# GpSimd kept in emission order, and the sixth product's weight splits two groups ahead, in a two-layer trunk kernel

## The chip, the cores and the metric

The kernel runs on one core of a Trainium2 chip. The metric is the device time of one launch in microseconds (us). The core's engines are TensorE (PE in the rows, PEld for its weight loads), VectorE (DVE), ScalarE (ACT), GpSimd (POOL) and SyncE (SP). DMAs are issued from an engine's instruction stream; those that GpSimd issues go through one queue, q0, and those of SyncE through q1.

## The reference

Two layers over 512 tokens of width 1024, in f32. Each layer makes one wide projection of the normed input, three token mixers (pooling, retention, attention into 256 memory tokens), merges them by gates, and ends with an output projection and a squared-ReLU MLP of width 4096:

```python
h = rms_norm(x, norm_mix_g[l])
proj = h @ w_in[l]
pool_u, rq, rk, rv, rg, xq, gates = split(proj)
y_pool = pool_mixer(pool_u, ...)
y_ret = retention(rq, rk, rv, rg, ...)
y_mem = memory_attention(xq, rms_norm(mem, mem_norm_g[l]), w_mem_kv[l])
merged = sum of sigmoid(gate_b) * (y_b @ w_up_b[l])
x = x + merged @ w_out[l]
h2 = rms_norm(x, norm_mlp_g[l])
x = x + square(relu(h2 @ w_mlp1[l])) @ w_mlp2[l]
```

## The kernel before

**Products.** Every big projection is a 1024x1024 weight against the 512 tokens, cut into 2x2 blocks, and computed with seven block products instead of eight. The code numbers them, and `products` (L293) runs them in the order 1, 2, 5, 3, 6, 4, 7. Each has two groups, for the two halves of the contraction; "4.1" here is product 4, second group. A layer runs, in this order, the projections v (with the first product of the next one taken ahead), qk, three gates (g1, g2, g0), the memory keys and values, rg, xq, three smaller up-projections without this scheme, w_out, and then four chunks of the MLP, each an mlp1 and an mlp2 projection.

**A group** takes a 512 KB weight tile `raw`, splits it into a high part (`wh`, a cast on ScalarE, L114) and a low part (`wl`, a subtraction on VectorE, L117), and multiplies with an operand that is split in the same way (`x6h` and `x6l` are the parts of product 6's operand; L104 and L105). Three matmuls stand for one (L123 to L125: wh with xh, wh with xl, wl with xh), so a group is 12 matmuls of 512 columns, or 24 of 256.

**Weights.** The weight's blocks are in three tiles per half, called A, C and B in the code. Sums of blocks are made in place by DMAs that add to SBUF, which GpSimd issues in `take`. After the splits 1.0 and 1.1 block (0,1) is added to A, after 5.0 and 5.1 block (1,1) is added to A, and after 3.0 and 3.1 block (0,1) is added to B (all L236). Product 6 takes A, and its `take` also adds A to C (L238, `raw<-raw`, SBUF to SBUF); product 4 takes that C. `skip` (L219) makes the first pair of adds where product 1 was done ahead. The plain loads of A, C and B are on SyncE's queue.

**Order.** `push` puts a group in a list; `prepare` emits the weight split of every group that is at most `look` places from the front, LOOK = 3 (2 for product 4). `MANUAL` names the engines whose instructions stay in the order in which the code emits them. It holds TensorE alone; on ScalarE, VectorE and GpSimd a scheduler sets the order when the program is built. `prep` emits a group's weight split, and after it the split of the operands that are to be had by then (`x.get`), or puts them on the list `wanted`. GpSimd also computes the inverse square roots of the norms (`pow`, L557): `yss` of retention's heads, which all come at the start of rg, `mr` of the memory, and `r` of the rows of `x`.

Of the kernel before, what the change touches and what calls it, by code (L numbers as in the profile page):

```python
# [2 lines left out]

# [13 lines left out]
ET = mybir.EngineType  # L17
# [16 lines left out]
MAGIC = 12582912.0  # L34
NSLOT = 72
LOOK = 3
MANUAL = {ET.PE}


C_CNT = 0  # L40
# [28 lines left out]
def tile_trunk(ctx, tc, a, out):  # L69
# [7 lines left out]
    psum = ctx.enter_context(tc.tile_pool(name="psum", bufs=8, space=PSUM))  # L77
    ctx.enter_context(tc.manual_schedule(engines=MANUAL))

    def slot(shape=(P, T), dt=F32, name="t"):  # L80
        return slots.tile(list(shape), dt, tag="t", name=name)

    def bank(name="ps"):
        return psum.tile([P, T], F32, tag="ps", name=name)
# [35 lines left out]
    def mm(ps, stat, mov, start, stop):  # L120

        (sh, sl), (mh, ml) = stat, mov
        nc.tensor.matmul(ps, sh, mh, start=start, stop=False, skip_group_check=True)  # L123
        nc.tensor.matmul(ps, sh, ml, start=False, stop=False, skip_group_check=True)  # L124
        nc.tensor.matmul(ps, sl, mh, start=False, stop=stop, skip_group_check=True)  # L125
# [15 lines left out]
    wanted = []  # L141
    follows = {1: (2,), 2: (5,), 5: (3, 4), 3: (6,), 6: (7,)}
# [17 lines left out]
    def prepare():  # L160
        for i, w in enumerate(queue):
            if w[0] and i <= w[2]:
                w[1], w[0] = w[0](), None

    def step():
        nonlocal post
        settle()
        _, state, _, go = queue.pop(0)
        post = go(state)
        prepare()  # L170

    def push(prep, go, look=LOOK):
        queue.append([prep, None, look, go])
        prepare()
        if len(queue) > LOOK:
            step()
# [6 lines left out]
    def urgent(f, *args):  # L183
        with tc.high_priority(offset=4000):
            return f(*args)
# [107 lines left out]
    def products(x, done, fm=False, last=False, acc=None, ahead=None):  # L293
# [9 lines left out]
        w, nxt = plan[at], plan[at + 1] if at + 1 < len(plan) else None  # L303
# [2 lines left out]
        ps = {}  # L306
        sb = {}

        def prep(p, kp, w=w):
            def f():  # L310
                wp = w.take(p, kp)
                for q in (p or 1, *follows.get(p, ())):
                    if x.have(q, kp):
                        for k in range(kp + 1):
                            if x.have(q, k):
                                x.get(q, k)
                    elif q == (p or 1):
                        wanted.append((x, q, kp))
                        break
                return wp  # L320

            return f

        def go(p, kp, into, new, fm=fm, then=None):
            def f(wp):
                if kp == 0 and new:
                    ps[into] = [bank(f"P{into}") for _ in range(2)]
                xp = x.get(p, kp)
                bs = ps[into]
                if fm:  # L330
                    for c in range(4):
                        o = bs[c // 2][:, (c % 2) * H:(c % 2 + 1) * H]
                        for k in range(2):
                            mm(o, tuple(v[:, k, c * P:(c + 1) * P] for v in wp), tuple(v[:, k, :] for v in xp),
                               new and kp == 0 and k == 0 and c % 2 == 0, kp == n - 1 and k == 1 and c % 2 == 1)
                else:
                    for b in range(2):
                        for k in range(2):
                            mm(bs[b], tuple(v[:, k, b * P:(b + 1) * P] for v in xp), tuple(v[:, k, :] for v in wp),
                               new and kp == 0 and k == 0, kp == n - 1 and k == 1)  # L340
                if kp == n - 1 and then:
                    return then
                if kp == n - 1:
                    return lambda: urgent(after, p) if p in (5, 6) or last and p in (3, 7) else after(p)

            return f
# [62 lines left out]

        def product(p, into=None):  # L410
            for kp in range(n):
                push(prep(p, kp), go(p, kp, into or p, into is None), LOOK - 1 if p == 4 else LOOK)

        def product_ahead(k, its_fm):
            its = plan[at - 1 + k]

            def then():
                for b in range(2):
                    u = slot(name="u2")
                    nc.scalar.copy(u, ps["ahead"][b])  # L420
                    early.setdefault(its, []).append(u)

            its.ahead()
            for kp in range(n):
                push(prep(0, kp, its), go(1, kp, "ahead", True, its_fm, then))

        if w.early:
            until(lambda: len(early.get(w, ())) == 2)
            for b, u in enumerate(early.pop(w)):
                sb["u", b] = u  # L430
            w.skip()
        else:
            product(1)
        if ahead:
            product_ahead(*ahead)
        product(2)
        if nxt:
            nxt.load("A")
        product(5)
        product(3)  # L440
        product(6, 5)
# [25 lines left out]
    def plain(xs, done):  # L467
# [33 lines left out]
        for c in range(2):  # L501
            for kp in range(n):
                push(prep(c, kp), go(c, kp))
# [271 lines left out]
    for l in range(DEPTH):  # L775
# [346 lines left out]
        def up_done(branch, first=False, final=False):  # L1122
# [17 lines left out]
            return done  # L1140

        products(hop, v_done, ahead=(1, True))
        products(hop, rotated, fm=True)
        sides.append(mixing())
        products(hop, gate_done(1))
        products(hop, gate_done(2))
        sides.append(memory())
# [141 lines left out]
```

## Time and profile before

| | |
|---|---|
| median of 3 runs | 1690.19 us (1690.08 to 1692.25) |
| the profiled execution, its own time | 1697.43 us |
| its span | 1695.4 us |
| mean granted TensorE clock | 0.986 of full |
| TensorE busy | 1614.6 us (95%) |
| VectorE busy | 1262.7 us (74%) |
| ScalarE busy | 1034.7 us (61%) |
| GpSimd busy | 313.6 us (18%) |

Shares are of the whole span, and stages with different limits lie in them. Busy time of GpSimd contains what it takes to issue a DMA, not the transfer. In the timelines below each row gives its start, its length, the engine, the line, the operation, what is written and read, and in brackets the engine's idle time before it and what ended that. A row of a `wh` cast that waits for `DMA raw<-raw` waits for the landing of an L238 copy into C.

### The profile page before, as it was taken

To read this page: it belongs to the slowest core of one execution; us is meant where nothing else is said; L and a number is where in the kernel's file an instruction comes from. 1 tells how busy PE (TensorE), PEld (TensorE's weight loads), DVE (VectorE), ACT (ScalarE), POOL (GpSimd) and SP (SyncE) were. 2 spreads that over 40 slices of the span, in tenths; PEclk is the share of its full clock that TensorE was granted. 3 is DMA by queue.
4 is the path that set the end of the run, shared out by engine and by line. 5 is a ranking of instruction groups with operands and counts; after the bars stand their busy time and mean duration, and the time that the engine had idled before them with its cause. 6 is when DMAs were issued, how large, how long until landed. Compare 5 with 4: busy or idle time off the path is not lost. (4 is left out here: it accounts for less than half of the span.)

```text
span 1695.4 us, 24850 instructions
## 1 busy us (share of the span) xinstructions
PE 1614.6 (95%) x9354; PEld 1419.1 (84%) x9354; DVE 1262.7 (74%) x1727; ACT 1034.7 (61%) x1655; POOL 313.6 (18%) x292
## 2 busy tenths in 40 slices
PE   6799999999989899999989999999999889999997
PEld 5697888998878888989868888889888688989895
DVE  4787675767687788696976876757757779796868
ACT  6456776646357656565765577756543577566565
POOL 2112212200012122222231223022000212222221
PEclk9999999999999899999999999999999999999999
DMA  8699986873666788988887999778435779888875
GB/s 237 148 229 235 251 211 148 183 232 103 193 128 126 162 195 178 197 189 207 180 200 159 241 242 244 218 169 181 151 115 162 173 160 186 194 177 189 174 151 123
DMA packets 155256, 311.16 MB, mean 184 GB/s; under 512 B 11320, under 2 KB 12544, under 8 KB 155136
## 3 DMA queue, kind: packets, MB, share of 16 engines
q0 software_dynamic: 61440, 134.23, 46.6%
q1 hardware_dynamic: 83872, 159.42, 28.0%
q10 hardware_dynamic: 9824, 15.93, 2.6%
q8 instruction: 73, 1.20, 0.3%
q14 instruction: 47, 0.39, 0.1%
HBM read 255.01 MB, written 16.78 MB: 160 GB/s over the span
## 5 line engine op out<-in xcount | busy, mean ns | idle before, releaser
L117 DVE TENSOR_TENSOR wl<-raw,wh 128x1024 fp32r<-128x1024 f32 x496 | 603.3, 1221 | 290.4 <-ACT wh L114 287.1
L114 ACT CAST wh<-raw 128x1024 fp32r<-128x1024 f32 x496 | 519.4, 1051 | 488.9 <-PE P L125 120.9
L236 POOL DMA_DIRECT2D raw<-in_w_mlp x92 | 121.6, 1352 | 386.3 <-DVE wl L117 250.2
L236 POOL DMA_DIRECT2D raw<-in_w_in x80 | 104.9, 1371 | 364.5 <-DVE wl L117 227.3
L238 POOL DMA_DIRECT2D raw<-raw x64 | 57.6, 900 | 168.9 <-DMA raw<-in_w_mlp 73.3
L1175 DVE TENSOR_TENSOR x<-x,P 128x512 f32<-128x512 f32 x120 | 78.3, 678 | 3.6 <-PE P L125 3.4
L123 PE MATMUL P<-wh,x6h 128*128 128x512 f32 x160 | 64.5, 403 | 10.4 <-ACT x6h L104 7.1
L123 PE MATMUL P<-wh,x3h 128*128 128x512 f32 x160 | 64.2, 401 | 10.0 <-ACT x3h L104 10.0
L125 PE MATMUL P<-wh,x6l 128*128 128x512 f32 x160 | 64.5, 403 | 4.3 <-DVE x6l L105 4.3
L236 POOL DMA_DIRECT2D raw<-in_w_out x12 | 15.9, 1461 | 275.6 <-DVE wl L117 156.1
L125 PE MATMUL P<-wh,x5l 128*128 128x512 f32 x160 | 63.5, 397 | 2.8 <-DVE x5l L105 2.8
L123 PE MATMUL P<-wh,x1h 128*128 128x512 f32 x160 | 64.1, 401 | 2.0 <-ACT x1h L104 2.0
L124 PE MATMUL P<-wl,x4h 128*128 128x512 f32 x160 | 62.8, 392 | 2.7 <-DVE wl L117 2.7
L125 PE MATMUL P<-wh,x3l 128*128 128x512 f32 x160 | 64.2, 401 | 0.3 <-DVE x3l L105 0.3
L124 PE MATMUL P<-wl,x6h 128*128 128x512 f32 x160 | 63.9, 399 | 0.6 <-DVE wl L117 0.6
L123 PE MATMUL P<-x6h,wh 128*128 128x256 f32 x192 | 56.5, 294 | 8.2 <-ACT P L368 8.2
L123 PE MATMUL P<-wh,x5h 128*128 128x512 f32 x160 | 63.3, 396 | 0.7 <-ACT x5h L104 0.5
L124 PE MATMUL P<-wl,x3h 128*128 128x512 f32 x160 | 63.8, 399 | 0.0
L123 PE MATMUL P<-wh,x7h 128*128 128x512 f32 x160 | 63.1, 394 | 0.5 <-ACT c L387 0.5
L124 PE MATMUL P<-wl,x1h 128*128 128x512 f32 x160 | 63.5, 397 | 0.0
L125 PE MATMUL P<-wh,x1l 128*128 128x512 f32 x160 | 63.2, 395 | 0.0
L123 PE MATMUL P<-wh,x4h 128*128 128x512 f32 x160 | 62.8, 393 | 0.1
(312 smaller groups left out, 5200.2 us busy)
## 6 DMA issues: line engine op xcount, KB each, us to landing
raw<-in_w_mlp SPq DMA_DIRECT2D x100, 512.0 KB, 5.0
raw<-in_w_mlp POOLq DMA_DIRECT2D x96, 512.0 KB, 7.6
raw<-in_w_in SPq DMA_DIRECT2D x88, 512.0 KB, 5.1
raw<-in_w_in POOLq DMA_DIRECT2D x84, 512.0 KB, 7.6
raw<-raw POOLq DMA_DIRECT2D x64, 512.0 KB, 6.8
sgl<-sig SPq DMA_DIRECT2D x48, 256.0 KB, 5.6
sig<-c ACTq DMA_DIRECT2D x36, 256.0 KB, 4.6
raw<-in_w_mem_kv SPq DMA_DIRECT2D x16, 512.0 KB, 5.5
```

What stands on the lines that cost most here:

```text
L114: nc.scalar.copy(hi, raw)
L117: nc.vector.tensor_tensor(lw, raw, hi.bitcast(F32), ALU.subtract)
L123: nc.tensor.matmul(ps, sh, mh, start=start, stop=False, skip_group_check=True)
L124: nc.tensor.matmul(ps, sh, ml, start=False, stop=False, skip_group_check=True)
L125: nc.tensor.matmul(ps, sl, mh, start=False, stop=stop, skip_group_check=True)
L236: nc.gpsimd.dma_start(raw, rows2(then, kp), accum_op=ALU.add)
L238: nc.gpsimd.dma_start(self.buf["C"][kp], raw, accum_op=ALU.add)
L1175: nc.vector.tensor_tensor(x, x, part, op)
```

## The change

GpSimd joins the engines that keep the order of emission. The weight splits of product 6 are emitted two groups ahead instead of three, as those of product 4 were already, and with them goes what `take` does after a split, the issue of the L238 DMA. The operand part of `prep` moves into a function of its own, which `push` runs when the group is put on the list, ahead of the weight split.

```diff
 LOOK = 3
-MANUAL = {ET.PE}
+MANUAL = {ET.PE, ET.Pool}
...
-    def push(prep, go, look=LOOK):
+    def push(prep, go, look=LOOK, first=None):
+        if first:
+            first()
         queue.append([prep, None, look, go])
         prepare()
...
+        def operands(p, kp):
+            for q in (p or 1, *follows.get(p, ())):
+                if x.have(q, kp):
+                    for k in range(kp + 1):
+                        if x.have(q, k):
+                            x.get(q, k)
+                elif q == (p or 1):
+                    wanted.append((x, q, kp))
+                    break
+
         def prep(p, kp, w=w):
-            def f():
-                wp = w.take(p, kp)
-                for q in (p or 1, *follows.get(p, ())):
...
-                return wp
-
-            return f
+            return lambda: w.take(p, kp)
...
-                push(prep(p, kp), go(p, kp, into or p, into is None), LOOK - 1 if p == 4 else LOOK)
+                push(prep(p, kp), go(p, kp, into or p, into is None), {6: 2, 4: 2}.get(p, LOOK), partial(operands, p, kp))
...
-                push(prep(0, kp, its), go(1, kp, "ahead", True, its_fm, then))
+                push(prep(0, kp, its), go(1, kp, "ahead", True, its_fm, then), LOOK, partial(operands, 0, kp))
```

The lines of the code move down by one to three: L236 becomes L239, L238 becomes L241, L557 becomes L558, L114 becomes L115.

On GpSimd in one mlp2 projection (layer 2, third chunk), from its first add to its last DMA; the tiles 15017 and 15019 are the halves of A, 15343 and 15345 those of B, 15215 and 15217 those of C. Before:

```order
L236 DMA raw_15017<-in_w_mlp2 128x2x512
L236 DMA raw_15019<-in_w_mlp2 128x2x512
L236 DMA raw_15017<-in_w_mlp2 128x2x512
L236 DMA raw_15019<-in_w_mlp2 128x2x512
L238 DMA raw_15215<-raw_15017 128x1024
L236 DMA raw_15343<-in_w_mlp2 128x2x512
L238 DMA raw_15217<-raw_15019 128x1024
L236 DMA raw_15345<-in_w_mlp2 128x2x512
```

And after the change:

```order
L239 DMA raw_15017<-in_w_mlp2 128x2x512
L239 DMA raw_15019<-in_w_mlp2 128x2x512
L239 DMA raw_15017<-in_w_mlp2 128x2x512
L239 DMA raw_15019<-in_w_mlp2 128x2x512
L239 DMA raw_15343<-in_w_mlp2 128x2x512
L239 DMA raw_15345<-in_w_mlp2 128x2x512
L241 DMA raw_15215<-raw_15017 128x1024
L241 DMA raw_15217<-raw_15019 128x1024
```

Both copies into C now stand behind both adds to B. The same holds in every projection of the scheme but xq, where the order was like this before.

On ScalarE in the same projection, after the change (before it, the rows stand in this order too), from the cast of 6.1 to that of 4.1:

```order
L115 CAST wh_15654<-raw_15019 128x1024
L105 CAST x4h_15534<-act_15462 128x512
L355 COPY u2_15543<-P1_15467 128x512
L355 COPY u2_15545<-P1_15468 128x512
L105 CAST x6h_15561<-xs6_15491 128x512
L115 CAST wh_15675<-raw_15215 128x1024
L105 CAST x6h_15582<-xs6_15526 128x512
L115 CAST wh_15693<-raw_15217 128x1024
```

Nothing moved here: the cast of 4.0, which reads C, stands ahead of the second `x6h`, as it did.

On GpSimd at the start of rg in the first layer; 2431 and 2433 are the halves of A. Before:

```order
L236 DMA raw_2431<-in_w_in 128x2x512
L557 TENSOR_TENSOR yss_2630<-yss_2630,nhalf_90 128x2
L236 DMA raw_2433<-in_w_in 128x2x512
L557 TENSOR_TENSOR yss_2680<-yss_2680,nhalf_90 128x2
L557 TENSOR_TENSOR yss_2732<-yss_2732,nhalf_90 128x2
L557 TENSOR_TENSOR yss_2766<-yss_2766,nhalf_90 128x2
L236 DMA raw_2431<-in_w_in 128x2x512
```

And after the change:

```order
L558 TENSOR_TENSOR yss_2630<-yss_2630,nhalf_90 128x2
L558 TENSOR_TENSOR yss_2680<-yss_2680,nhalf_90 128x2
L558 TENSOR_TENSOR yss_2732<-yss_2732,nhalf_90 128x2
L558 TENSOR_TENSOR yss_2766<-yss_2766,nhalf_90 128x2
L239 DMA raw_2431<-in_w_in 128x2x512
L239 DMA raw_2433<-in_w_in 128x2x512
L239 DMA raw_2431<-in_w_in 128x2x512
```

All four `yss` now stand ahead of the first add of rg. The order of TensorE and of SyncE is the same before and after.

## Rows read from the trace of the kernel before

**Rows 1.** The page's head, and its line of the weight subtractions (count, busy, mean ns).

```profile
span 1695.4 us, 24850 instructions
PE 1614.6 (95%) x9354; PEld 1419.1 (84%) x9354; DVE 1262.7 (74%) x1727; ACT 1034.7 (61%) x1655; POOL 313.6 (18%) x292
...
L117 DVE TENSOR_TENSOR wl<-raw,wh 128x1024 fp32r<-128x1024 f32 x496 | 603.3, 1221 | 290.4 <-ACT wh L114 287.1
```

**Rows 2.** Waits by engine and releaser: us in total, times, longest us.

```profile
PE P L123 <- ACT x3h L104: 11.1, 4, 6.4
PE P L123 <- ACT x6h L104: 7.1, 2, 3.8
PE P L125 <- DVE x6l L105: 4.3, 2, 2.4
...
ACT wh L114 <- DMA raw<-raw: 95.3, 33, 6.4
```

**Rows 3.** The page's DMA queues: packets, MB, share of 16 engines' span.

```profile
q0 software_dynamic: 61440, 134.23, 46.6%
```

**Rows 4.** Timeline, xq: GpSimd's first adds after 5.0; ScalarE's cast 4.0; both layers.

```profile
327.79 3.69 POOL L236 DMA_DIRECT2D raw<-in_w_in  x3 [9.64 <-DVE wl L117]
...
345.06 1.05 ACT L114 CAST wh<-raw 128x1024 fp32r<-128x1024 f32 x1 [6.36 <-DMA raw<-raw]
...
1159.17 3.68 POOL L236 DMA_DIRECT2D raw<-in_w_in  x3 [10.18 <-DVE wl L117]
...
1175.31 1.05 ACT L114 CAST wh<-raw 128x1024 fp32r<-128x1024 f32 x1 [5.42 <-DMA raw<-raw]
```

**Rows 5.** Timeline, mlp2, layer 2, third chunk: GpSimd, ScalarE, VectorE and TensorE.

```profile
1570.44 1.20 POOL L236 DMA_DIRECT2D raw<-in_w_mlp  x1 [7.29 <-DVE wl L117]
...
1585.21 1.07 ACT L114 CAST wh<-raw 128x1024 fp32r<-128x1024 f32 x1
...
1590.13 2.01 ACT L114 CAST wh<-raw 128x1024 fp32r<-128x1024 f32 x2 [3.34 <-DMA raw<-raw]
...
1588.63 0.68 DVE L105 TENSOR_TENSOR x6l<-xs,x6h 128x512 fp32r<-128x512 f32 x1
...
1590.20 0.39 PE L125 MATMUL P<-wh,x6l 128*128 128x512 f32 x1
```

**Rows 6.** Timeline, rg: GpSimd and TensorE in layer 1, then in layer 2.

```profile
281.66 0.69 POOL L557 TENSOR_TENSOR yss<-yss,nhalf 128x2 f32<-128x2 f32 x1 [1.88 <-DVE yss L556]
285.77 1.23 POOL L236 DMA_DIRECT2D raw<-in_w_in  x1 [3.43 <-DVE wl L117]
...
292.10 0.91 POOL L238 DMA_DIRECT2D raw<-raw  x1 [2.37 <-DMA raw<-in_w_in]
...
307.45 0.39 PE L124 MATMUL P<-wl,x4h 128*128 128x512 f32 x1
...
1113.24 0.69 POOL L557 TENSOR_TENSOR yss<-yss,nhalf 128x2 f32<-128x2 f32 x1 [1.95 <-DVE yss L556]
...
1138.83 0.39 PE L124 MATMUL P<-wl,x4h 128*128 128x512 f32 x1
```

**Rows 7.** Timeline, w_out of layer 2: GpSimd's add after 5.0, ScalarE's cast 4.0, TensorE.

```profile
1310.15 1.21 POOL L236 DMA_DIRECT2D raw<-in_w_out  x1 [14.34 <-DVE wl L117]
...
1328.06 1.04 ACT L114 CAST wh<-raw 128x1024 fp32r<-128x1024 f32 x1
...
1331.16 0.80 PE L123 MATMUL P<-wh,x6h 128*128 128x512 f32 x1 [3.79 <-ACT x6h L104]
```

**Rows 8.** Windows (window, length; busy us of PE, PEld, DVE, ACT, POOL; PEclk, DMA share, GB/s).

```profile
850.00:860.00 10.00, 7.78 (x43) 6.37 (x42) 8.24 (x13) 7.18 (x14) 3.15 (x3) 1.00 1.01 241
1331.00:1338.00 7.00, 4.94 (x11) 3.49 (x12) 6.78 (x11) 3.02 (x7) 0.00 (x0) 0.52 0.98 238
```

**Rows 9.** Timeline, between the layers: GpSimd's `r` and TensorE's first transpose behind it.

```profile
851.03 1.20 POOL L557 TENSOR_TENSOR r<-r,nhalf 128x2 f32<-128x2 f32 x1
...
853.41 0.76 PE L454 MATMUL tr<-ident,xn 128*128 128x128 f32 x5 [2.22 <-ACT xn L586]
```

More of the change, by code (lines that the diff above doesn't have):

```diff
@@ L2 @@
 from fractions import Fraction
+from functools import partial
 import concourse.bass as bass
@@ L307, in products @@
         sb = {}
-        def prep(p, kp, w=w):
-            def f():
-                wp = w.take(p, kp)
-                for q in (p or 1, *follows.get(p, ())):
[L313 to L319, printed above, removed]
-                return wp
-            return f
+        def operands(p, kp):
[7 more added lines that the diff above has]
+                    break
+        def prep(p, kp, w=w):
+            return lambda: w.take(p, kp)
         def go(p, kp, into, new, fm=fm, then=None):
```

## The prediction, made before the changed kernel ran

> **What bounds the kernel now.** The page's head first: TensorE is busy for 1614.6 of 1695.4 us [rows 1]. Its order does not change and nothing is taken from its work, so the change can only win or lose idle time of TensorE, 81 us in all, and the clock that goes with it. The list of waits says what of that is near this change [rows 2]: TensorE stands 11.1 us for `x3h`, 7.1 for `x6h` and 4.3 for `x6l`. The same list shows a wait that costs little so far: 33 of the 64 `wh` casts behind a C copy stand on ScalarE for it, 95.3 us in all. Last the queue: q0 is busy 46.6% of the span [rows 3], over 192 adds and 64 copies, so a transfer of 512 KB takes 0.466 x 1695.4 / 256 = 3.1 us of all 16 engines, and as GpSimd's transfers follow one another in it, what stands ahead of a copy is paid by who waits for the copy.
>
> **The change part by part.**
>
> Nothing is removed or added: the same instructions, with GpSimd's in another order. What moves are the C copies (L238). Before, most projections had them right behind the 5.0 and 5.1 adds or between the B adds; now both B adds come first. 4.0's cast, which reads C, waits for four adds and a copy behind 5.0's split. That arrangement is already there in xq, and there the time from the issue of 5.0's add to 4.0's cast, which ended a wait for the copy, was 345.06 - 327.79 = 17.27 us and 1175.31 - 1159.17 = 16.14 us [rows 4].
>
> *mlp2, eight times.* In the third chunk of layer 2 the 5.0 add is issued at 1570.44 and 4.0's cast starts at 1585.21 without a wait [rows 5]. Behind that cast on ScalarE stands the second `x6h`, and behind its subtraction on VectorE the second `x6l` (the order shows it for ScalarE; on VectorE it is the same in all mlp2 but the last of a layer). From the cast to the end of `x6l` it takes 1.05 + 1.22 + 0.68 = 2.95 us [rows 1, 4, 5], and TensorE wants `x6l` at 1590.20 [rows 5]. So the cast is harmless up to 1587.25. At xq's pace it comes at 1570.44 + 16.14 to 17.27 = 1586.58 to 1587.71: nothing to 0.5 us. The pace of this projection itself is another: 4.1's cast, which today has three adds and two copies ahead of it in q0, five transfers as 4.0's will have (four adds and its copy), came at 1590.13, 19.69 us behind the issue. By that 4.0 would be late by 2.9 us. I take 2.0, nearer to the projection's own row than to xq's, because the weight slices and the load on the queues are its own; in the last chunk of each layer, where `x6l` stands ahead of 4.0's subtraction, 1.2 less, 0.8. Sum 6 x 2.0 + 2 x 0.8 = **13.6 us** (0 to 20.8). mlp1 has its 4.0 cast due later relative to 5.0 (groups of 24 matmuls, and no second `x6h` held up that TensorE wants at once); I put it at nothing, and the same holds of g2, g0 and qk; what hides it there is the product 6 still running on TensorE, and if that cover were short by a microsecond in each of eight mlp1, 8 us would come on top.
>
> *rg, twice.* The four `yss` now stand ahead of rg's first add. The last one runs at 281.66 for 0.69, so 1.0's add is issued at 282.35 or later; 5.0's split must wait for it to land. An add there took 292.10 - 285.77 = 6.33 us to land, as the C copy waiting for it shows [rows 6]. Then come cast and subtraction, 1.05 + 1.22 = 2.27 us, and 5.0's add is issued at 290.95, not 285.77. With 17.27 us behind it 4.0's cast starts at 308.22. TensorE wants `wl` of 4.0 at 307.45, so the latest harmless start was 305.18: late by 3.0. In layer 2, 1113.24 + 0.69 + 6.33 + 2.27 + 17.27 = 1139.80 against 1138.83 - 2.27 = 1136.56: 3.2. Sum **6.3 us** (4.0 at 16.14, 11.2 at 19.69).
>
> *w_out, twice.* The 5.0 add is issued at 1310.15, 4.0's cast starts at 1328.06, `x6h` stands behind it, and TensorE waits 3.79 us for that [rows 7]. The 5.1 add, which waited behind a copy that itself waited for 5.0's landing, now goes earlier, but `x6h` will stand behind 4.0's cast all the same, at 1310.15 + 16.14, 17.27 or 19.69 = 1326.3, 1327.4 or 1329.8. That is -1.8, -0.7 or +1.8 each. I take +1.0, sum **+2.0** (-3.6 to +3.6).
>
> *v, g1, m10.* In the first layer's v the `x3h` stall of 6.4 us, the longest of its row [rows 2], stands behind a 6.1 cast that waits for the 5.1 add; that add now leaves before the copy, worth up to one transfer of 3.1 us: -2.5 (-5.3 to -1). In the second layer's v the second `x6h` moves behind 4.1's cast, one more copy of 3.1 us to wait for, part hidden: +1.5 (-1 to +3). g1's 4.0 is among the 33 waiting casts, of 2.9 us on average (95.3 / 33) [rows 2], half of that as my estimate for one layer: +1.5 (0 to 5.8). mlp1's first chunk (m10): 0 (-2.5 to +3). Sum **+0.5**.
>
> *`r`, three times.* Between layers, and from w_out to the MLP, `r` now stands ahead of an add issue. `r` ran at 851.03, 0.76 us after that issue began, on which it waited, and the first transpose behind it is what TensorE idled 2.22 us for [rows 9]: 3 x -0.76 = **-2.3**.
>
> *The clock.* From 1331 to 1338 the granted clock was 0.52, the 1.2 GHz level, behind two stalls of 3.79 and some 2 us [rows 7, 8]: 7 x 0.48 = 3.4 us lost. Behind the lone 2.22 us of the layer boundary it stayed at 1.00 [rows 8, 9]. So a stall of 2 us need not cost it and one of 4 may. I take half of the loss, 1.7, for each rg and for two of the eight mlp2: **+6.8** (0 to 17).
>
> Sum 13.6 + 6.3 + 2.0 + 0.5 - 2.3 + 6.8 = **+26.9 us**. The profiled execution took 1697.43 us, its span 1695.4 and 2.0 around it; that becomes 1724.3. It is 7.2 above the median of the runs, so the median goes from 1690.19 to **1717**. All low ends together give about -10 (1680), all high ends about +62 (1752).
>
> The trace gives 3.1 us for a transfer in q0 [rows 3]. The Trainium skill, "DMA: Bandwidth & Descriptors", section "Anatomy of one DMA — SWDGE (gpsimd) path", fits such a DMA at 2.0 us that don't grow plus its bytes over 436e3 per us; if the fixed part of one overlaps the next, 512 KB would be an estimated 1.2 us each and the two B adds 2.4 us together. By that the copies would hardly be later, and the time would go rival A's way; the trace's 3.1 us speaks against it.
>
> **The rivals.**
>
> *A, faster, about 1665.* The adds freed from the copies (5.1 no longer behind a copy that waits for 5.0) end the waits of TensorE for `x3h`, `x6h` and `x6l`, 11.1 + 7.1 + 4.3 = 22.5 us, and `r` brings 2.3: 1690.2 - 24.8 = 1665. Place: w_out, v and m10. It decides if the two B adds ahead of a copy cost it less than 1587.25 - 1585.21 = 2.0 us together, so that no 4.0 cast in mlp2 gets late. For it: these stalls are real and adds are in them. Against it: 3.1 us each by the queue's share, and xq's 16 to 17 us.
>
> *B, nearly unchanged, about 1692.* xq's faster pace holds everywhere: mlp2 0 to 4, rg 4 to 6, w_out -2, v -1, g1 0, `r` -2.3, no clock loss, +2 in the middle. This is also the case in which the move of product 6 has no effect of its own, since the order of ScalarE in mlp2 is what it was. For it: xq is the very arrangement. Against it: the mlp2 row of 19.69.
>
> *C, much slower, about 1741.* The projection's own pace holds: mlp2 6 x 2.9 + 2 x 1.7 = 20.8, rg 11.2, w_out 3.6, v and g1 +0.5, `r` -2.3, and the clock falls behind each of the ten stalls, 17: +50.8. For it: the fall after w_out. Against: no fall after 2.22 us.
>
> **How the numbers follow.** Forecast 0.58, A 0.16, B 0.12, C 0.14. About 0.2%, 3.4 us, is what a measurement of this kernel can tell from no change. Of B, 0.07 lies within that, 0.03 above and 0.02 below. Faster: 0.16 + 0.02 = 0.18; same 0.07; slower 0.58 + 0.14 + 0.03 = 0.75. The range reaches from the middle of B's band below, 1687, to 1748, above C's middle; it leaves out most of A and a part of C, some 0.2.
>
> **What would show it.** Right: ScalarE's wait of `wh` for `raw<-raw` well above 95.3 us; TensorE waiting some 2 us for `x6h` or `x6l` in each mlp2, about eight new waits, and for `wh` or `wl` of 4.0 in both rg; 4.0's casts in mlp2 starting 17 to 20 us behind the issue of the 5.0 add; the clock below 1.00 behind some of them; the transposes behind `r` idling 0.7 us less. Wrong: 4.0's casts in mlp2 without a wait and the `x3h` and `x6h` waits gone (A), or new waits of ScalarE that TensorE does not feel (B). It is also wrong if the stalls come somewhere else, in mlp1 above all, which I put at nothing.

## The result, and the profile after

The changed kernel takes 1751.59 us (median of four runs, 1748.0 to 1757.66) against 1691.22 us before: **3.5% slower**, ratio 1.0348 with a 95% interval of 1.0326 to 1.037. The forecast was 1717 us in 1687 to 1748. The sign was right, the loss more than twice as large as forecast (60.4 us between the medians, 26.9 forecast), and the median lies 3.6 us above the range.

The page of the profiled execution, its first lines and its queue line, for [rows 1] and [rows 3]:

```profile
span 1752.1 us, 24907 instructions
...
PE 1633.1 (93%) x9354; PEld 1427.9 (81%) x9354; DVE 1260.1 (72%) x1727; ACT 1034.4 (59%) x1655; POOL 315.0 (18%) x292
...
q0 software_dynamic: 61440, 134.23, 44.3%
```

The span grew by 56.7 us. TensorE's busy time grew by 18.5 of them although it does the same 9354 matmuls: a third of the loss is matmuls that run slower behind a stall. The other 38.2 us are idle time. The queue moves the same bytes. The waits, for [rows 2] (us in total, times, longest); the first line is one of before that [rows 2] does not have:

```profile
PE P L123 <- ACT P L368: 11.6, 4, 4.1
...
PE P L124 <- ACT P L369: 27.6, 4, 7.9
PE P L124 <- ACT x6h L105: 18.4, 10, 6.3
...
PE P L124 <- ACT wh L115: 8.9, 4, 2.9
PE mtr L958 <- ACT mnf L961: 8.6, 2, 4.3
PE P L125 <- DVE wl L118: 7.4, 6, 2.2
PE P L126 <- DVE x6l L106: 6.9, 8, 1.6
PE P L124 <- ACT x3h L105: 4.8, 3, 3.2
...
ACT wh L115 <- DMA raw<-raw: 181.0, 56, 8.4
```

56 of the 64 casts of product 4 now wait for their C copy, 181.0 us in all (33 casts and 95.3 us before). TensorE feels it in several forms: ten waits for `x6h` instead of two, eight for `x6l` instead of two, four for `wh` itself (4.0 of both rg and both g1), a new kind, `mnf` (a step of the memory norm, 8.6 us), and a longer wait for `P` (the copy of product 5's sum out of its bank, L369, which product 6 overwrites), 27.6 us instead of 11.6.

Where the loss lies follows from the start of each projection's first matmul in the two traces (TensorE's order is the same, so each can be paired). Time added between the start of a projection and that of the next, us, first and second layer, beside the terms of the forecast:

| place | measured | forecast |
|---|---|---|
| six inner mlp2 | 1.6, 2.0, 1.8; 1.9, 1.9, 1.9 (sum 11.1) | 12.0 |
| last mlp2 of a layer | 1.6; 5.9 | 1.6 |
| rg | 5.6; 5.8 | 6.3, and 3.4 for the clock |
| w_out | 2.2; 2.6 | 2.0 |
| g0 | 5.2; 5.2 | 0 |
| v | 3.5; 1.5 | -1.0 |
| g1 | 2.0; 3.3 | 1.5 |
| first mlp1 chunk (m10) | 0.1; 3.0 | 0 |
| qk, g2, other mlp1 | 0.0 each | 0 |
| xq up to w_out | 0.0; -1.9 | 0 |

The parts sum to 56.7 us. The forecast's sum of 26.9 holds besides these 3.4 us of clock in two of the eight mlp2 and -2.3 us for `r`. The 1.9 us won between xq and w_out are won in every kernel below; no term had them.

**mlp2.** The third chunk of layer 2 after the change, timeline of GpSimd, ScalarE and TensorE, for [rows 5], then the window from 6.1 to the end of product 6 (length; busy us of PE, PEld, DVE, ACT, POOL; PEclk, DMA share, GB/s):

```profile
1619.31 1.20 POOL L239 DMA_DIRECT2D raw<-in_w_mlp  x1 [6.86 <-DVE wl L118]
...
1628.44 2.33 POOL L241 DMA_DIRECT2D raw<-raw  x2
...
1637.87 1.05 ACT L115 CAST wh<-raw 128x1024 fp32r<-128x1024 f32 x1 [3.72 <-DMA raw<-raw]
1638.82 0.61 ACT L105 CAST x6h<-xs 128x512 fp32r<-128x512 f32 x1
...
1639.48 0.50 PE L124 MATMUL P<-wh,x6h 128*128 128x512 f32 x1 [0.76 <-ACT x6h L105]
...
1640.83 0.50 PE L126 MATMUL P<-wh,x6l 128*128 128x512 f32 x1 [0.61 <-DVE x6l L106]
...
1638.50:1643.20 4.70, 3.33 (x13) 2.28 (x13) 4.25 (x6) 3.45 (x5) 0.00 (x0) 1.00 0.75 225
```

4.0's cast starts 18.56 us behind the issue of the 5.0 add, having waited for the copy; the second `x6h` stands behind it, and TensorE stalls twice at 6.1. The granted clock stays at 1.00, the 2.4 GHz level, through both stalls.

**rg**, first layer: the last `yss` root, the first adds, 4.0's cast, TensorE's wait for it, and the window of the group 4.0 (columns as above), for [rows 6]:

```profile
292.26 0.69 POOL L558 TENSOR_TENSOR yss<-yss,nhalf 128x2 f32<-128x2 f32 x1 [1.89 <-DVE yss L557]
292.90 2.48 POOL L239 DMA_DIRECT2D raw<-in_w_in  x2
...
319.57 1.04 ACT L115 CAST wh<-raw 128x1024 fp32r<-128x1024 f32 x1 [8.30 <-DMA raw<-raw]
...
320.67 0.50 PE L124 MATMUL P<-wh,x4h 128*128 128x512 f32 x1 [2.65 <-ACT wh L115]
321.93 0.50 PE L125 MATMUL P<-wl,x4h 128*128 128x512 f32 x1 [0.76 <-DVE wl L118]
...
320.67:326.13 5.46, 4.70 (x12) 3.52 (x13) 4.21 (x5) 2.94 (x4) 0.00 (x0) 0.69 0.84 267
```

The stall at the start of 4.0 adds 2.8 us, which was forecast as 3.0. As much again is lost in the group itself: from its start to that of 4.1 it took 5.46 us instead of 2.72. TensorE waits 0.76 us for `wl` in it, and at a mean granted clock of 0.69, part of it at the 1.2 GHz level, 0.31 x 5.46 = 1.7 us of it go to the clock.

**g0**, first layer: the memory norm's roots `mr` between GpSimd's DMAs, ScalarE, and TensorE:

```profile
226.97 0.57 POOL L558 TENSOR_TENSOR mr<-mr,nhalf 128x1 f32<-128x1 f32 x1 [4.07 <-DVE mr L557]
...
231.96 0.58 POOL L558 TENSOR_TENSOR mr<-mr,nhalf 128x1 f32<-128x1 f32 x1 [3.16 <-DVE mr L557]
232.50 1.94 POOL L241 DMA_DIRECT2D raw<-raw  x2
...
237.99 1.05 ACT L115 CAST wh<-raw 128x1024 fp32r<-128x1024 f32 x1 [6.50 <-DMA raw<-raw]
...
243.32 0.83 ACT L961 ACTIVATE mnf<-mtr,gains 128x256 f32<-128x256 f32 x2
...
244.21 1.11 PE L958 MATMUL mtr<-ident,mi 128*128 128x128 f32 x4 [4.34 <-ACT mnf L961]
```

Here the copies are behind two roots as well as two adds. GpSimd waits 4.07 and 3.16 us for VectorE's part of the roots, with the adds and copies queued behind. 4.0's cast waits 6.50 us, `mnf` stands behind it and three more weight casts, and TensorE, whose next instruction is the next transpose of the memory, waits 4.34 us for that. One of the three, the cast of 7.1, stood behind `mnf` before: the scheduler moved it on ScalarE, for about 1.0 us of the delay.

**v**, second layer: ScalarE, VectorE and TensorE:

```profile
913.32 1.05 ACT L115 CAST wh<-raw 128x1024 fp32r<-128x1024 f32 x1 [2.06 <-DMA raw<-raw]
...
917.24 1.04 ACT L115 CAST wh<-raw 128x1024 fp32r<-128x1024 f32 x1 [0.35 <-DMA raw<-raw]
...
918.32 1.23 DVE L118 TENSOR_TENSOR wl<-raw,wh 128x1024 fp32r<-128x1024 f32 x1 [0.70 <-ACT wh L115]
...
920.07 1.28 DVE L188 TENSOR_TENSOR c<-u,P 128x512 f32<-128x512 f32 x2
920.78 1.17 ACT L369 COPY P<-P 128x512 f32<-128x512 f32 x2 [1.97 <-DVE c L188]
...
921.40 0.79 PE L124 MATMUL P<-wh,x6h 128*128 128x512 f32 x1 [6.80 <-ACT P L369]
...
921.40:929.35 7.95, 7.95 (x24) 6.36 (x25) 3.95 (x6) 2.83 (x4) 0.00 (x0) 0.68 0.61 223
```

The 5.1 add did get free, and product 3's second group starts earlier. But behind it 4.0's cast, the copies `u`, 4.1's subtraction, the sums `c` and the copy `P` follow one another, and 6.0 waits 6.80 us for the last of them. The last row is the window of product 6 behind that wait: no stall is left in it, and its matmuls took 7.95 us instead of 5.57, at a granted clock of 0.68. (In the first layer it was 8.46 us instead of 5.58, at 0.64.) A wait of 1.7 us for `q` earlier in the second layer's v is gone in every kernel below and hides a part of this.

**w_out**, second layer, the add behind 5.0, 4.0's cast and TensorE's wait, for [rows 7]:

```profile
1349.64 1.21 POOL L239 DMA_DIRECT2D raw<-in_w_out  x1 [14.33 <-DVE wl L118]
...
1370.07 1.04 ACT L115 CAST wh<-raw 128x1024 fp32r<-128x1024 f32 x1 [6.04 <-DMA raw<-raw]
...
1373.18 0.80 PE L124 MATMUL P<-wh,x6h 128*128 128x512 f32 x1 [6.31 <-ACT x6h L105]
```

20.4 us lie between the add and the cast, more than the 16.1 to 19.7 us that the forecast allowed for.

### The profile page after: what moved, and what is told of

Its sections match the earlier page's. It is cut to its first block, busy times and chain, and to the rows that moved or that the text cites. A ratio compares the mean times of both kernels' runs of the same rounds, so it can differ in the third digit from the quotient of the medians.

```text
span 1752.1 us, 24907 instructions
## 1 busy us (share of the span) xinstructions
PE 1633.1 (93%) x9354; PEld 1427.9 (81%) x9354; DVE 1260.1 (72%) x1727; ACT 1034.4 (59%) x1655; POOL 315.0 (18%) x292
## 4 chain that ended last, share of the span: by engine, by line
issue 42%; PE 29%; DMA 15%; POOL 6%; DVE 5%; ACT 3%; POOLq 0%; SPq 0%; ACTq 0%; DVEq 0%
PE P L125 7%; PE P L126 6%; PE P L124 6%; DMA raw<-in_w_mlp 5%; DMA raw<-raw 5%; DMA raw<-in_w_in 4%; POOL raw L239 3%; DVE wl L118 2%; POOL raw L241 2%; ACT wh L115 1%; PE up L126 1%; PE up L125 1%; PE up L124 1%; PE kv L124 1%; PE kv L125 1%
## 5 line engine op out<-in xcount | busy, mean ns | idle before, releaser
L115 ACT CAST wh<-raw 128x1024 fp32r<-128x1024 f32 x496 | 516.5, 1050 | 513.9 <-DMA raw<-raw 181.0
L239 POOL DMA_DIRECT2D raw<-in_w_mlp x92 | 111.4, 1236 | 478.9 <-DVE wl L118 347.8
L239 POOL DMA_DIRECT2D raw<-in_w_in x80 | 97.5, 1256 | 346.0 <-DVE wl L118 283.6
L124 PE MATMUL P<-wh,x6h 128*128 128x512 f32 x160 | 68.4, 428 | 31.3 <-ACT x6h L105 18.4
L124 PE MATMUL P<-wh,x4h 128*128 128x512 f32 x160 | 67.6, 422 | 8.9 <-ACT wh L115 8.9
L125 PE MATMUL P<-wl,x4h 128*128 128x512 f32 x160 | 67.9, 424 | 7.4 <-DVE wl L118 7.4
L241 POOL DMA_DIRECT2D raw<-raw x64 | 71.7, 1360 | 8.2 <-DMA raw<-in_w_in 7.0
L124 PEld LDWEIGHTS P<-wh,x6h 128*128 128x128 f32 x160 | 32.7, 205 | 42.7 <-ACT x6h L105 22.6
L126 PE MATMUL P<-wh,x4l 128*128 128x512 f32 x160 | 66.6, 416 | 0.0
L239 POOL DMA_DIRECT2D raw<-in_w_out x12 | 14.5, 1209 | 284.6 <-DVE wl L118 167.1
```

The source lines that it names most:

```text
L115: nc.scalar.copy(hi, raw)
L239: nc.gpsimd.dma_start(raw, rows2(then, kp), accum_op=ALU.add)
L241: nc.gpsimd.dma_start(self.buf["C"][kp], raw, accum_op=ALU.add)
```

## The experiments

The theory after these rows: the loss comes from what now stands ahead of the C copies, and of rg's first adds, on GpSimd. The rivals: the shorter look-ahead of product 6; that the place of the copies matters little beside the roots and the clock; and, for mlp2, that TensorE lacks product 4's weights rather than `x6h`. Held still by no run is what the scheduler moved on ScalarE and VectorE together with the new order, in g0, in rg and between the layers.

The shorter look-ahead and the earlier operands without the order on GpSimd need no run: the program built with these two alone has the same order on all engines as the kernel before.

**The order on GpSimd alone.** An edit of the kernel before:

```diff
-MANUAL = {ET.PE}
+MANUAL = {ET.PE, ET.Pool}
```

> The kernel before with GpSimd kept in emission order and nothing else (product 6 still three groups ahead, operands still behind the weight split). Theory (the loss comes from the place of the C copies, the row roots and the adds on GpSimd): the C copies stand behind both B adds here too, so the time is that of the changed kernel, 1747 to 1757 us. Rival 1 (it is the shorter look-ahead of product 6): 1690 to 1700 us.

Measured: 1752.45 us, ratio 1.0346 (1.0314 to 1.0377), that of the whole change. (Each ratio here is against runs of the kernel before that were made beside it, 1693.39 us for this and the next three kernels, 1693.78 for the last three.) Product 6 is pushed behind the B adds' splits, so even at three groups ahead its copies are emitted behind both adds. The look-ahead and the operands explain nothing of the total. By place the two kernels differ: here g0 loses 7.8 and 6.8 us, rg 7.0 and 6.3, and the last mlp2 of layer 2 2.8 instead of 5.9.

**The copies ahead of the B adds.** An edit of the changed kernel:

```diff
+            if p == 3:
+                nc.gpsimd.dma_start(self.buf["C"][kp], self.buf["A"][kp], accum_op=ALU.add)
             if then is not None:
                 nc.gpsimd.dma_start(raw, rows2(then, kp), accum_op=ALU.add)
-            if p == 6:
-                nc.gpsimd.dma_start(self.buf["C"][kp], raw, accum_op=ALU.add)
```

> The changed kernel with each C copy issued right ahead of the B add of the same half, so that GpSimd's order in a projection is 5.0 5.1 copy 3.0 copy 3.1, as in most projections of the kernel before. Theory: the mlp2, v, w_out and g1 losses go (some 20.8, 6.9, 5.1 and 5.3 us), the two rg keep theirs (5.6 and 5.8, by the yss roots ahead of the first adds) and the two g0 a part (one copy still behind one mr root): 1695 to 1708 us. Rival 1 (look-ahead) or rival 2 (the falling clock and other queues): little changes, 1740 us or more.

Measured: 1682.74 us, ratio 0.9938 (0.9923 to 0.9954): faster than the kernel before, and below the expected 1695. By place against the kernel before, the inner mlp2 lose nothing (-0.3 to 0.0 us), rg keeps only 1.5 and 1.1 us, g0 0.0 and 2.0, and v (-1.2, -0.7), w_out (-3.8, -3.7), g1 of the first layer (-2.4) and the first m10 (-3.9) win. Moving the 64 copies takes back the loss and more. What was missed in the expectation: in v, w_out and m10 the 5.1 add stays freed from the first copy, which is the gain that the fast rival of the prediction described.

**One B add ahead of the first copy instead of two.**

```diff
+            if p == 3 and kp == 1:
+                nc.gpsimd.dma_start(self.buf["C"][0], self.buf["A"][0], accum_op=ALU.add)
             if then is not None:
                 nc.gpsimd.dma_start(raw, rows2(then, kp), accum_op=ALU.add)
-            if p == 6:
+            if p == 6 and kp == 1:
```

> The changed kernel with one B add instead of two ahead of the first C copy: 5.0 5.1 3.0 copy 3.1 copy. Theory: 4.0's cast in mlp2 comes one transfer, about 2.9 us, earlier, 15.7 us behind the issue of the 5.0 add instead of 18.6, under the 16.8 from which it costs; the mlp2 losses of 1.9 us each go, rg keeps most; 1705 to 1725 us in all. If the loss grew evenly with each add, half of it would stay: 1720 us and mlp2 losses of 1 us each.

Measured: 1730.55 us, ratio 1.0211 (1.0191 to 1.0231), a little above the expected 1705 to 1725. The same mlp2 chunk, and below it g0 of the first layer:

```profile
1600.65 1.20 POOL L241 DMA_DIRECT2D raw<-in_w_mlp  x1 [6.54 <-DVE wl L118]
...
1615.60 1.06 ACT L115 CAST wh<-raw 128x1024 fp32r<-128x1024 f32 x1 [0.25 <-DMA raw<-raw]
...
224.32 0.57 POOL L560 TENSOR_TENSOR mr<-mr,nhalf 128x1 f32<-128x1 f32 x1 [4.43 <-DVE mr L559]
224.86 1.04 POOL L239 DMA_DIRECT2D raw<-raw  x1
```

4.0's cast in mlp2 comes 14.95 us behind the issue of the 5.0 add instead of 18.56: 3.6 us for one add less. From product 6 to product 7 five of the six inner mlp2 lose nothing and the sixth 0.2 us (three lose 0.4 to 1.7 us elsewhere in the projection, the largest at 7.1, which was not followed up), so the loss of mlp2 does not grow evenly with the adds; it begins somewhere between these two, as the prediction had it (16.8 us). rg keeps 4.7 and 5.4 us.

g0 still loses 7.1 and 5.0 us, although one B add less is ahead of its first copy: that copy still stands behind one root, and the second behind both, and now 4.1's cast, ahead of `mnf` too, waits 6.21 us. With the order of the run before, where the first copy is ahead of both roots and the second behind one, g0 lost 0.0 and 2.0. The roots alone were not moved in any run, but the run of the order alone tells the two roots apart: in layer 2 its first copy, behind both adds, is ahead of the second root, where the changed kernel has it behind. GpSimd and 4.0's cast there:

```profile
1087.16 1.22 POOL L236 DMA_DIRECT2D raw<-in_w_in  x1
1087.91 1.39 POOL L238 DMA_DIRECT2D raw<-raw  x1
1091.52 0.57 POOL L557 TENSOR_TENSOR mr<-mr,nhalf 128x1 f32<-128x1 f32 x1 [2.21 <-DVE mr L556]
...
1097.76 1.05 ACT L114 CAST wh<-raw 128x1024 fp32r<-128x1024 f32 x1 [6.70 <-DMA raw<-raw]
```

The second add and 4.0's cast in the changed kernel:

```profile
1083.92 1.22 POOL L239 DMA_DIRECT2D raw<-in_w_in  x1
...
1094.27 1.05 ACT L115 CAST wh<-raw 128x1024 fp32r<-128x1024 f32 x1 [6.38 <-PE P L126]
```

The cast came 10.60 us behind the second add there and 10.35 in the changed kernel: the second root did not make it late. What is left is the first root, for which GpSimd stands some 4 us before it issues the second add, and the B adds ahead of the copies; how the 5 us divide between them no run shows.

**rg's first adds ahead of the last three roots.**

```diff
-        until(lambda: all(y[t][hp] is not None for t in range(NT) for hp in range(2)))
+        halves, w_rg = [0, 1], plan[at]
+        while not all(y[t][hp] is not None for t in range(NT) for hp in range(2)):
+            step() if queue else settle()
+            if halves and len(queue) <= 2:
+                kp = halves.pop(0)
+                w_rg.ready[1, kp] = w_rg.take(1, kp)
```

> The changed kernel with the two first adds of rg (and their weight splits) emitted before the last three yss roots; TensorE's order is the same. Theory: rg's loss goes, 5.6 and 5.8 us, since its 5.0 split is no longer held up and 4.0's cast comes some 313.7 us into the run where TensorE wants it at 315.6: 1738 to 1744 us. Rival (in rg too the two B adds alone make the loss): 1749 us or more, rg's 4.0 still late by 2 us or more in each layer.

Measured: 1737.64 us, ratio 1.026 (1.0239 to 1.0282). rg loses 0.0 us in both layers. The first add of rg, the 5.0 add, and 4.0's cast in the first layer:

```profile
277.99 1.22 POOL L239 DMA_DIRECT2D raw<-in_w_in  x1
...
295.80 1.23 POOL L239 DMA_DIRECT2D raw<-in_w_in  x1 [3.43 <-DVE wl L118]
...
313.37 1.05 ACT L115 CAST wh<-raw 128x1024 fp32r<-128x1024 f32 x1 [5.28 <-DMA raw<-raw]
```

The cast came at 313.37, expected at 313.7; it still waits 5.28 us for its copy, and TensorE does not feel it. With the B adds ahead of the copy and the first adds early rg loses nothing; with the first adds held and the copies ahead of the B adds it lost 1.5 and 1.1; only the two together cost 5.6 and 5.8. The stall gone, the slow clock behind it is gone too (1.00 from 312 to 327).

**The second `x6` on VectorE.** The C copies stay where the change put them.

```diff
+                if p == 6 and kp == 1:
+                    v = self.value(p, kp)
+                    hi, lw = slot((P, T), F32R, name="x6h"), slot((P, T), F32R, name="x6l")
+                    nc.vector.tensor_copy(hi, v)
+                    nc.vector.tensor_tensor(lw, v, hi.bitcast(F32), ALU.subtract)
```

> The changed kernel with the high part of product 6's second operand half made by VectorE (a copy of 0.6 us, in front of 4.0's weight subtraction there) instead of ScalarE; the C copies stay behind both B adds. Theory (in mlp2 the late C copy costs only because the second x6h stands behind 4.0's cast on ScalarE): the six inner mlp2 projections lose 0 to 0.5 us each instead of 1.6 to 2.0, and 4.0's cast starts as late as before, some 18.6 us behind the issue of the 5.0 add; rg, g0 and g1 keep their losses (5.6, 5.2, 2 to 3 us); 1735 to 1745 us in all. Rival (TensorE waits for 4.0's own weights): the 1.9 us only move from 6.1 to 4.0, 1750 us.

Measured: 1760.19 us, ratio 1.0391 (1.0373 to 1.0409), slower than the changed kernel and outside the expectation. TensorE in the third chunk of layer 2, then 4.0's cast in the last chunk:

```profile
1649.97 0.50 PE L126 MATMUL P<-wh,x6l 128*128 128x512 f32 x1 [1.49 <-DVE x6l L293]
...
1657.10 0.50 PE L125 MATMUL P<-wl,x4h 128*128 128x512 f32 x1 [1.62 <-DVE wl L118]
...
1730.46 1.06 ACT L115 CAST wh<-raw 128x1024 fp32r<-128x1024 f32 x1 [3.91 <-DMA raw<-raw]
```

The scheduler put the new copy ahead of 4.0's subtraction on VectorE, but in the six inner mlp2 it left `x6l` behind it, so that TensorE waits for `x6l` instead of `x6h`; and it put 4.1's subtraction behind eleven other instructions, a second stall. That makes 3.7 to 5.5 us each between product 6 and product 7. So these six don't answer the question. The last chunk of each layer does in part: there both instructions stand ahead of 4.0's subtraction, 4.0's cast stands idle for 3.6 and 3.9 us ahead of its start (3.6 and 4.9 in the changed kernel), and product 6 to product 7 takes 0.6 us less than in the kernel before, where the changed kernel lost 3.8 and 5.0 us. A late copy alone did not cost there. (Product 7 itself and what follows it lost 3.7 and 1.7 us, of which the cause stays open.) Other instructions of VectorE moved there as well, so this supports the chain through `x6` rather than proves it; no run takes nothing but the second `x6` out of the wait.

**Both mends together**, the edits of the second and the fourth run:

> Both mends in the changed kernel: each C copy right ahead of the B add of its half, and rg's two first adds ahead of the last three yss roots. Theory: the gain of the first alone (1683 us) and rg's rest of 1.5 and 1.1 us: 1678 to 1682 us. Rival (the two are not independent, rg's rest comes from the order of the copies): 1683 us as without.

Measured: 1678.27 us, ratio 0.9906 (0.9893 to 0.9919). This is the fastest, 0.9% below the kernel before, as expected. Its waits for copies:

```profile
ACT wh L115 <- DMA raw<-raw: 78.7, 27, 5.4
```

27 casts wait for copies, fewer than before; rg loses 0.0, g0 0.4 us each, w_out wins 2.5 and 3.7.

**Both copies at once behind the 5.1 add**, with rg's adds early:

```diff
             if then is not None:
                 nc.gpsimd.dma_start(raw, rows2(then, kp), accum_op=ALU.add)
-            if p == 6:
-                nc.gpsimd.dma_start(self.buf["C"][kp], raw, accum_op=ALU.add)
+            if p == 5 and kp == 1:
+                for k in range(2):
+                    nc.gpsimd.dma_start(self.buf["C"][k], self.buf["A"][k], accum_op=ALU.add)
```

> The changed kernel with both C copies right behind the 5.1 add, ahead of both B adds, and rg's two first adds early. Theory (what counts is how many transfers stand ahead of a copy): 4.0's and 4.1's casts come earlier still, but 3.1's B add later, and GpSimd waits for 5.0's landing with the B adds behind it; 7.0's cast needs those; 1676 to 1686 us. Rival: 7.0's cast gets late by the B adds and this is slower than with the copies between them, 1690 us or more.

Measured: 1688.49 us, ratio 0.9973 (0.9958 to 0.9988). The casts' waits for copies nearly vanish (10.0 us in all), yet it is slower than with the copies between the adds, and above the expectation. v and w_out win more (v -4.6 in the first layer, w_out -5.3 in the second), but g0 loses 5.8 and 5.6 us, now waiting for VectorE's `mi`, and one mlp2 3.6. There VectorE's part of the second root comes late, and the root runs 30.1 us into g0 instead of 24.2, in the first layer. The order of VectorE and ScalarE moved in this kernel too; why the part is late stays open. The copies at their earliest are not the optimum.

## Why the prediction was half right

Two steps failed above all: the one that put g0 at nothing ("the same holds of g2, g0 and qk"), where the runs showed 10.4 us, and the clock's term, 6.8 us, where TensorE's busy time grew by 18.5.

**The mechanism held.** The C copies behind both B adds, 4.0's cast waiting on ScalarE, the second `x6h` behind it: the inner mlp2 lost 11.1 us where 12.0 was forecast, and the cast came 18.56 us behind the 5.0 add, between xq's 17.27 and the projection's own 19.69, as 2.0 us each lies between the 0.5 and 2.9 that these two gave. qk, g2 and seven of eight mlp1 at nothing held as well (0.0 each); only m10 of the second layer lost 3.0. That the cast is harmless up to some 16.8 us is borne out as far as the runs go: at 14.95 us, with one add less, it cost nothing, at 18.56 it did.

**The price of a transfer held.** q0's share after the change, 0.443 x 1752.1 / 256, is 3.0 us a transfer, and one add less ahead of a copy brought the cast 3.6 us earlier. The 1.2 us estimated from the fit in the Trainium skill ("DMA: Bandwidth & Descriptors", "Anatomy of one DMA — SWDGE (gpsimd) path") does not agree with either. At 3 us a transfer the fast rival fell, but only as long as the B adds are ahead: its gain in v, w_out and m10 is real, as the run with the copies ahead of the B adds showed.

**g0 at nothing was the largest error, 10.4 us.** The copies went behind the roots `mr` there, and I looked only at whether 4.0's cast would be late for product 4. The step that failed is "the same holds of g2, g0": work of another stage (`mnf`) stands behind the same cast, and TensorE, in strict order, wanted that first. With the copies ahead of the B adds and the first of them ahead of the roots the loss was 0.0 and 2.0 us. The roots and the adds both moved in that run, and their shares stay open.

**v had the wrong sign**, 5.0 us lost for -1.0. The freed 5.1 add did end part of the `x3h` wait (4.8 us in all instead of 11.1). What I did not follow is the rest of ScalarE's queue in v: `u` behind 4.0's cast, `c` behind 4.1's subtraction, and the copy `P` behind `c`, for which 6.0 waits. That wait was in the trace of before as `P`, and I read only the `x3h` rows. Nor did I price the clock behind it: product 6 alone took 2.9 and 2.4 us longer.

**The last mlp2 of a layer was undersized.** I gave it 0.8 each because `x6l` stands ahead of 4.0's subtraction; measured 1.6 and 5.9. There 4.1's subtraction is late as well: TensorE waits 2.16 us for it in both layers, where it waited 0.77 before, which no term had. In the first layer part of the loss comes back at the layer boundary. The 5.9 us are not a fixed price: the run with rg's adds early has the same order there, and lost 2.5.

**g1 and w_out** had the right cause and were priced too low: 5.3 for 1.5 (it was priced for one layer, and half of a wait), 4.8 for 2.0 (20.4 us to the cast, not 17 to 19.7).

**The clock's term was far too small.** Where I had put it, it was about right: in rg the group 4.0 lost 1.7 us to the clock in each layer, as forecast, and of the eight mlp2 two lost some, the last of each layer (0.89 and 0.90 over the 16.1 and 17.3 us from product 6 to product 7). In the other six it did not fall. But it fell where I had counted nothing (first layer, mean over the projection: v from 0.95 to 0.90, w_out 0.93 to 0.90, g1 1.00 to 0.96, g0 1.00 to 0.97). TensorE's busy time, for the same matmuls, grew by 18.5 us for the 6.8 of the term.

**`r`** was put at -2.3. The two waits between w_out and the MLP shrank by 0.1 us each, not 0.76 (1.44 to 1.33 and 1.45 to 1.33); only the one at the layer boundary, 2.22 us, went. The sum is -2.4, so the size came out by luck. At the boundary, too, 1.1 us of the wait stayed in five of the other kernels with GpSimd in order.

The sum missed by 29.8 us (56.7 less 26.9). By place, g0, v and the last mlp2 make 22.3 of them; by kind, 11.7 are slower matmuls (18.5 less 6.8), within these and other places, and the rest is idle time.

## What to carry to other kernels

When an in-order queue gets a new order, list for every transfer that moves back the instruction that waits for it, and then everything queued behind that instruction on its engine, whatever stage it belongs to; the consumer that stalls is often not the one the transfer was for. Small computations (norm roots) and DMA issues in one strict order hold each other: in g0 a root that waited 4 us for VectorE held an add and the copies behind it, in a projection that lost 5 us. A stall also costs the matmuls behind it where the clock falls, here a third of the whole loss. And where an order by hand loses, an order by hand in between can beat both: putting each copy right ahead of the add that need not be early was worth 0.6% over the scheduler's order, and 0.9% with rg's first adds early.

## What the runs showed of the hardware that I had not expected

Stalls of 2.65 and 0.76 us, 1.3 us from start to start, came with a mean granted clock of 0.69 over their group in rg, while two of 0.76 and 0.61 us, 1.4 us apart in the same way, left it at 1.00 in mlp2.

DMA issues on ScalarE's stream held it for 5 us. In v of the first layer, after the change, two small loads of the positions stood in ScalarE's stream between two casts:

```profile
55.89 5.05 ACTq L651 DMA_DIRECT2D posi<-in_positions  x2
60.98 0.62 ACT L105 CAST x6h<-xs 128x512 fp32r<-128x512 f32 x1 [8.03 <-DMA posi<-in_positions]
```

Before the change the same two issues took 1.17 us. They now begin 1.2 us earlier, but an early start alone does not make them long: in the seven other kernels, which all have GpSimd in order, the two took 1.57 to 5.42 us, and the shortest of these began earlier still, at 52.68. What makes them long stays open. The copy `P` for which TensorE waits 6.2 us at 6.0 in v of the first layer stands behind them on ScalarE.
